# Hybrid layer on one core: the lower part of one weight piece per gate/up chunk by ScalarE and an adding DMA, other steps moved

## The chip, the core and the metric

The kernel runs on one core of a Trainium2 chip. TensorE (PE) multiplies 128x128 blocks, VectorE (DVE) and ScalarE (ACT) work on 128 partitions, GpSimd (POOL) and SyncE (SP) issue DMAs here. The metric is the device time of one execution in microseconds (us); lower is better. Times are compared as medians of several runs.

## The reference

One layer on 256 tokens of width 2048, all in float32: a feed-forward block, a mixer (retention heads and sparse attention beside each other), a second feed-forward block, each added to x, and a last norm. The part that fills most of the time is the feed-forward block, run twice with 5632 hidden columns:

```
def rmsnorm(x, g):
    y = xf * lax.rsqrt(jnp.mean(xf * xf, axis=-1, keepdims=True) + NORM_EPS)
    return (y * g.astype(jnp.float32)).astype(x.dtype)

def swiglu(h, w_gate, w_up, w_down):
    return (jax.nn.silu(h @ w_gate) * (h @ w_up)) @ w_down

x = x + 0.5 * swiglu(rmsnorm(x, ffn1_norm), ffn1_w_gate, ffn1_w_up, ffn1_w_down)
... mixer: rope on queries and keys, retention, top-64 attention, x + concat @ w_out
x = x + 0.5 * swiglu(rmsnorm(x, ffn2_norm), ...)
return rmsnorm(x, final_norm)
```

## The kernel before, in words

**Two parts of every number.** TensorE multiplies in a rounded form of float32. To keep the precision, every operand is held as an upper part `hi` (the rounded number, written by an ACT copy, L287) and a lower part `lo` (the number less `hi`, a DVE subtraction, L293). A product takes three matmuls: hi with hi, hi with lo, lo with hi.

**Pieces.** All weights stream from HBM in loads of 1 MB into three buffers `raw` (`load`, L259). A load is cut into pieces of at most 1024 columns; `split` (L268) makes `hi` and `lo` of one piece, and the matmuls of a piece follow. A feed-forward block is cut into chunks of 512 hidden columns; `wide` (L179) lists the pieces of one chunk, which hold gate and up side by side. A pair is 256 rows of the weights, one load. A plain pair (C) has two pieces and 24 matmuls. A pair of kind S replaces the 2x2 block product by seven products of sums: DVE first subtracts quarters of the raw weights in place (`less`, L278), and there are four pieces and 21 matmuls. A chunk is eight pairs. All chunks but the first of each block follow `UP` in the order `ORDER`, that is S C S C S C C C, with 22 pieces; there are 20 of them, five in each of the two parts of the two blocks. A down pass (`DOWN`) follows each part, in two halves.

**Order of the work.** The program fixes the order on every engine. The main loop (L1072 to L1085) goes over the pieces: at step i it runs the small tasks booked for that step (`after`, `run_step`; a task that yields n goes on n steps later), then splits piece i + 4, then issues the matmuls of piece i. `hi` and `lo` have five buffers each, so the split of a piece waits until the piece five before it has been multiplied. A load is issued when the buffer of the load three before it is free, which is when DVE has made the last `lo` of it.

**What is booked in a chunk.** Once the last S pair is multiplied, `sums_of` (L479) puts the seven products together: ACT copies bank M1, DVE adds M6 to it (L477); one step later the transposes of the chunk before go into M1 and M6 (`turn`, L563, with L567) and are split again; one step later DVE adds M5 and M7. Half a chunk's end later `ups` and `hidden` (L542, L550) add the plain products, apply silu on ACT and multiply.

**Other places that the change touches.** `tables` (L650) makes the sine and cosine tables on DVE and ACT during the first down pass and sends them through DRAM. `turn_early` (L592) transposes x at the end of the first block. `rstd` and `row_of` (L457, L439) turn the norm's factor into a row by a matmul with `diag`; `scaled_tables` (L710) multiplies the tables by it; `rope` (L731) uses them. `rg_done` (L813) makes the gates of the retention heads and `ret_mix` (L993) combines them with the heads' output for `w_out`. `FIRST` (L32) is the order of the pairs in the very first chunk, in which x is also scaled, transposed and split (`first_x`, and for S pairs `s_of_x`, L362).

Of the kernel before, what the change touches and what calls it, by code (L numbers as in the profile page):

```python
# [19 lines left out]
P = 128  # L20
# [8 lines left out]
UP = "CSCSCSCC"  # L29
ORDER = (1, 0, 3, 2, 5, 4, 6, 7)  # L30
PLAIN = "CCCCCCCC"
FIRST = (0, 2, 4, 6, 7, 1, 3, 5)  # L32
DOWN = ("SCSCSCSCCCCC", "SCSCSCSCCC")
NH = 8
NI = 16
# [16 lines left out]
def layer(ctx: ExitStack, tc: tile.TileContext, a: dict, out: bass.AP):  # L52
# [18 lines left out]
    def half_k(tag, bufs=2):  # L71
        return new(tmp, [P, 2, T], F32, tag, bufs)
# [35 lines left out]
    def after(step, fn):  # L108
        ends.setdefault(step, []).append(fn)
# [68 lines left out]

    def wide(src, plan, left, x0=False, tail=False, order=None, sums=SUM):  # L179

        start = len(pieces)
        seen, last = {}, {}
        ending = [[], []]
        s_end = None

        def mm(i, off, a, m, at=None, p=None):

            for n, (u, v) in enumerate(((0, 0), (0, 1), (1, 0))):
                st = m not in seen
                seen[m] = 1  # L190
                e = [i, off, (pieces[i]["pair"], a), m, u, v, st, False]
                last[m] = e
                pieces[i if at is None else at]["mms"].append(e)

        for at, p in enumerate(order or range(len(plan))):
            kind = plan[p]
            loads.append([(0, block(src, 2 * at, 2 * at + 2, 1024))])
            if x0:
                loads[-1] = [lambda p=p: load_xT(p)] + [(o, loads[-1][0][1][:, o:o + n]) for o, n in
                                                        ([(0, 512), (512, 512), (1024, 1024)] if at == 0 else [(0, 2048)])]  # L200
            i = len(pieces)
            if kind == "C":
                tiles = [(0, 1024), (1024, 1024)]
                if x0 and at == 0:
                    tiles = [(0, 512), (512, 512), (1024, 1024)]
            else:
                tiles = [(512, 1024), (1024, 1024), (0, 1024), (1536, 512)]
            for k, (off, n) in enumerate(tiles):
                pieces.append(dict(load=len(loads) - 1, off=off, n=n, mms=[], left=left, pair=p,
                                   sums=k if kind == "S" else None, x=[p] if x0 and k == 0 else []))  # L210
            if kind == "C":
                for c in (1, 0):
                    for k in range(2):
                        off = 1024 * (1 - c) + 512 * k
                        j = max(j for j, (o, n) in enumerate(tiles) if o <= off)
                        for t in range(2):
                            if tail and p >= len(plan) - 2:
                                ending[t].append((i + j, off - tiles[j][0], p, (t, k), sums[f"{t + 1}{c + 1}"]))
                                continue
                            mm(i + j, off - tiles[j][0], (t, k), sums[f"{t + 1}{c + 1}"])  # L220
            else:
                for k, off, a, m in S_BLOCKS:
                    mm(i + k, off, a, m)
                s_end = len(pieces)

        ending[1].sort(key=lambda e: e[4], reverse=True)
        for t in range(2):
            for i, off, p, a, m in ending[t]:
                mm(i, off, a, m, i if t == 0 else len(pieces) - 1)
        for e in last.values():  # L230
            e[7] = True
        return start, s_end, len(pieces) - 1, len(pieces)
# [22 lines left out]
        return len(pieces)  # L255

    n_loaded = [0]

    def load(i):  # L259
        raws[i] = new(wts, [P, 2048], F32, "raw", 3)  # L260
# [7 lines left out]
    def split(i):  # L268
        p = pieces[i]
        while n_loaded[0] < min(len(loads), p["load"] + 3):  # L270
            load(n_loaded[0])
            n_loaded[0] += 1
        for c in p.get("x", []):
            first_x(c, xT.pop(c))
        r = raws[p["load"]]
        raw = r[:, p["off"]:p["off"] + p["n"]]

        def less(a, b, o):  # L278
            V.tensor_tensor(r[:, o:o + 512], r[:, a:a + 512], r[:, b:b + 512], op=OP.subtract)  # L279


        k = p.get("sums")
        if k == 1:
            less(0, 1024, 1024)
        hi = new(wts, [P, 1024], F32R, "hi", BUFS)
        lo = new(wts, [P, 1024], F32R, "lo", BUFS)
        S.activation(hi[:, :p["n"]], raw, AF.Copy)  # L287
        if k == 1:
            less(0, 512, 0)
            less(512, 1024, 512)  # L290
        elif k == 2:
            less(1536, 512, 1536)
        V.tensor_tensor(lo[:, :p["n"]], raw, hi[:, :p["n"]].bitcast(F32), op=OP.subtract)  # L293
        split_of[i] = (hi, lo)


    def gain(norm, c, j):
# [141 lines left out]
    def row_of(tok):  # L439

        diag = new(tmp, [P, 2, P], F32, "diag", 1)
        for t in range(2):
            V.tensor_scalar(diag[:, t], ident, tok[:, t:t + 1], None, op0=OP.mult)
        ps = small()
        yield 2
        for t in range(2):
            TE.matmul(ps[:, t * P:(t + 1) * P], lhsT=ones, rhs=diag[:, t], start=True, stop=True)
        return ps[:, :T]
# [77 lines left out]
    def ffn(which, norm, next_norm, last):  # L526
        wgu, wd = a[f"wgu{which}"], [a[f"wd{which}{j}"] for j in range(2)]
        c = 0
        for part, n in enumerate(PARTS):
            hs = {}  # L530
            marks[which, part] = len(pieces)
            for cc in range(n):
                plain = c == 0
                start, s_end, half, end = wide(wgu[c], PLAIN if plain else UP, left_of(xg if plain else xs),
                                               plain and which == 1,
                                               order=ORDER if not plain else FIRST if which == 1 else None)
                u = {}

                if not plain:
# [51 lines left out]

    def turn_early(s_end, norm):  # L592

        for i, m in enumerate(("M1", "M5", "M6", "M7")):
            after(s_end + 2 + i, lambda i=i, m=m: turn_x(i, norm, m))

    def turn_late(end, norm, banks, later=0):
# [49 lines left out]

    rot_dram = new(dram, [P, 4, T], F32, "rot_dram")

    def tables():  # L650
        for k in range(2):
            ang, n = half_k("b"), half_k("sq")
            pi, pf = n[:, 0].bitcast(I32), n[:, 1]
            G.dma_start(pi, bass.AP(tensor=a["pos"].tensor, offset=a["pos"].offset, ap=[[0, P], [1, T]]))
            yield 4
            V.tensor_copy(pf, pi)
            for j in range(2):
                V.tensor_scalar(ang[:, j], pf, inv[:, k:k + 1], None, op0=OP.mult)
            yield 2
            V.tensor_scalar(n, ang, 1.0 / C_TWO_PI, None, op0=OP.mult)  # L660
            V.tensor_scalar(n[:, 0], n[:, 0], 0.25, None, op0=OP.add)
            yield 2
            V.tensor_scalar(n, n, MAGIC, None, op0=OP.add)
            V.tensor_scalar(n, n, MAGIC, None, op0=OP.subtract)
            for c in (C1, C2, C3):
                yield 2
                V.scalar_tensor_tensor(ang, n, -c, ang, op0=OP.mult, op1=OP.add)
            yield 1
            V.tensor_scalar(ang[:, 0], ang[:, 0], math.pi / 2, None, op0=OP.add)
            yield 1  # L670

            V.tensor_scalar(n, ang, 1.0 / C_TWO_PI, MAGIC, op0=OP.mult, op1=OP.add)
            V.tensor_scalar(n, n, MAGIC, None, op0=OP.subtract)
            for c in (C1, C2, C3):
                yield 2
                V.scalar_tensor_tensor(ang, n, -c, ang, op0=OP.mult, op1=OP.add)
            yield 2
            V.tensor_scalar(ang, ang, PI_DOWN, -PI_DOWN, op0=OP.min, op1=OP.max)
            yield 2
            S.activation(ang, ang, AF.Sin)  # L680
            yield 2
            V.tensor_scalar(ang[:, 1], ang[:, 1], sgn[:, k:k + 1], None, op0=OP.mult)
            G.dma_start(rot_dram[:, 2 * k:2 * k + 2], ang)
        yield 1
        act_table(AF.Silu)

    def load_tables():
        mix_ext()
# [12 lines left out]

    after(FIRST_SQ, first_squares)
    end = ffn(1, 0, 1, False)
    after(marks[1, 0, "down"] + 1, tables)
    after(marks[1, 1, "down"] + 4, load_tables)


# [6 lines left out]
        yield 2  # L714
        V.tensor_tensor(rot[:, :2], rot[:, :2], two(r_of[1]), op=OP.mult)

    after(m0 + 3, scaled_tables)

    heads = {}
    done_at = {}  # L720
# [26 lines left out]
    def cols(name, src, nchunks, idx=False, first=False):  # L747
# [7 lines left out]
        for c in range(nchunks):  # L755
            chunk = chunks[c]
            end = ends_[c] if c in ends_ else stream(src[c], kts, 256, 8, 4, rhs_x, chunk, mm_cols, 2)

            def done(chunk=chunk, c=c):
                if c % 2 == 0:  # L760
                    heads[name].append(big(shape=(P, 4, T)))
                return rope(chunk, 2, heads[name][c // 2][:, 2 * (c % 2):2 * (c % 2) + 2], idx,
                            3 if len(heads) == 1 and c == 0 else 1)

            after(end, done)
        done_at[name] = len(pieces)
# [42 lines left out]
    for c in range(4):  # L809
# [3 lines left out]
        def rg_done(chunk=chunk, c=c):  # L813
# [3 lines left out]
            s = half_k("s")  # L817
            S.activation(s, g, AF.Silu)
            gate[c] = s

        after(end, rg_done)
        rg_end.append(end)
# [213 lines left out]
    after(s + 6, ret_norm)  # L1036
    for n in range(2):
        after(s + 7 + n, lambda n=n: ret_scale(n))
    for c in range(4):
        after(max(rg_end[c] + 2, s + 10 + 2 * c), lambda c=c: ret_mix(c))  # L1040

    class MixIn:
# [129 lines left out]
```

## Time and profile before

| | |
|---|---|
| median of 3 runs | 1867.61 us (1867.21 to 1868.33) |
| the profiled execution | 1868.15 us, of it the span from first to last instruction 1866.3 us |
| PE busy | 98% of the span, 8643 matmuls |
| DVE busy | 88%, ACT 57%, POOL 0.4% |
| DMA | 360.51 MB, mean 193 GB/s |
| mean granted clock of PE | 0.997 |

An engine's idle time is shown before the instruction that it waited with, and the releaser is the instruction whose end let it go on. Busy times of PE are modelled: a matmul of 512 columns is drawn with 0.39 us, but such matmuls start 0.23 us apart.

### The profile page before, as it was taken

What the parts mean: (1) busy time and instruction counts of PE and PEld (TensorE: products, weight loads), DVE (VectorE), ACT (ScalarE), POOL (GpSimd) and SP (SyncE); (2) the same over time, 40 slices, a digit from 0 to 9 for tenths busy, and PEclk for the clock granted to TensorE, in tenths of its full rate; (3) what the DMA queues carried; (4) which work ended last, traced back from release to release, by engine and by line L of the source; (5) the groups of instructions that cost most, each with busy time, mean ns of one, the idle gap of its engine ahead of it and who ended that gap; (6) DMA issues with size and microseconds to landing.
All of it is one profiled execution on the core that took longest, in us unless ns stands there. A gap on an engine that the chain in (4) does not pass through costs nothing.

```text
span 1866.3 us, 22800 instructions
## 1 busy us (share of the span) xinstructions
PE 1836.9 (98%) x8643; PEld 1523.8 (82%) x8643; DVE 1646.2 (88%) x2122; ACT 1072.9 (57%) x1353; POOL 6.9 (0%) x17
## 2 busy tenths in 40 slices
PE   9999999999999999999999999999999999999997
PEld 7788787888888887988888888888888888888886
DVE  6999999999999997689865886799999889999997
ACT  7655655545565555656554566556555455555564
POOL 0000000000000000000000000000000000000000
PEclk9999999999999999999999999999999999999999
DMA  8545555565554544545434464555555555555454
GB/s 316 203 181 183 203 203 191 180 229 198 205 206 183 212 181 173 184 159 210 179 137 172 145 225 150 207 185 191 210 207 183 202 203 198 186 188 212 186 190 170
DMA packets 52237, 360.51 MB, mean 193 GB/s; under 512 B 5984, under 2 KB 5984, under 8 KB 9632
## 3 DMA queue, kind: packets, MB, share of 16 engines
q1 hardware_dynamic: 50976, 355.62, 51.6%
q0 software_dynamic: 576, 1.84, 0.3%
q10 hardware_dynamic: 576, 1.60, 0.3%
q8 instruction: 67, 1.10, 0.2%
q14 instruction: 42, 0.34, 0.1%
HBM read 356.42 MB, written 2.62 MB: 192 GB/s over the span
## 4 chain that ended last, share of the span: by engine, by line
PE 80%; DVE 12%; ACT 4%; issue 2%; DMA 2%; SPq 0%; ACTq 0%; DVEq 0%
PE M L236 63%; PE M L150 8%; DVE lo L293 7%; PE M L152 4%; DVE raw L279 2%; ACT hi L287 2%; PE M L168 1%; PE M L169 1%; PE M L167 1%; PE M L567 1%; DMA raw<-in_wgu 1%; DMA e<-in_xT 1%; DVE x L474 1%; ACT sq L416 0%; DVE e L477 0%
## 5 line engine op out<-in xcount | busy, mean ns | idle before, releaser
L287 ACT ACTIVATE hi<-raw 128x1024 fp32r<-128x1024 f32 (+2 forms) x859 | 844.6, 1006 | 561.5 <-DVE raw L279 359.5
L293 DVE TENSOR_TENSOR lo<-raw,hi 128x1024 fp32r<-128x1024 f32 (+2 forms) x859 | 976.4, 1159 | 122.1 <-ACT hi L287 108.7
L236 PE MATMUL M<-hi,xg 128*128 128x512 f32 x2240 | 725.5, 390 | 1.7 <-ACT e L546 1.5
L236 PE MATMUL M<-hi,mid 128*128 128x512 f32 x1690 | 527.4, 391 | 1.9 <-DVE e L1001 1.6
L236 PEld LDWEIGHTS M<-hi,xg 128*128 128x128 f32 x2240 | 420.5, 188 | 89.2 <-ACT e L546 1.9
L236 PE MATMUL M<-lo,xg 128*128 128x512 f32 x1120 | 437.9, 391 | 5.7 <-DVE lo L293 5.6
L236 PEld LDWEIGHTS M<-hi,mid 128*128 128x128 f32 x1690 | 317.2, 188 | 70.2 <-DVE e L1001 2.0
L236 PE MATMUL M<-lo,mid 128*128 128x512 f32 x845 | 329.8, 390 | 1.0 <-DVE lo L293 0.8
L279 DVE TENSOR_TENSOR raw<-raw 128x512 f32<-128x512 f32 x380 | 262.9, 692 | 12.7
L236 PEld LDWEIGHTS M<-lo,xg 128*128 128x128 f32 x1120 | 210.3, 188 | 55.5 <-DVE lo L293 12.7
L150 PE MATMUL M<-xg,hi 128*128 128x512 f32 x688 | 245.6, 401 | 0.4 <-DVE xg L307 0.3
L236 PEld LDWEIGHTS M<-lo,mid 128*128 128x128 f32 x845 | 158.6, 188 | 36.5 <-DVE lo L293 4.3
L152 PE MATMUL M<-xg,lo 128*128 128x256 f32 x645 | 180.9, 280 | 0.0
L150 PEld LDWEIGHTS M<-xg,hi 128*128 128x128 f32 x688 | 128.7, 189 | 30.3 <-issue 1.3
L236 PE MATMUL M<-hi,ext 128*128 128x512 f32 x360 | 141.2, 392 | 1.5 <-ACT s L557 1.4
L152 PEld LDWEIGHTS M<-xg,lo 128*128 128x128 f32 x645 | 122.3, 190 | 0.8
L236 PEld LDWEIGHTS M<-hi,ext 128*128 128x128 f32 x360 | 67.5, 188 | 18.9 <-DVE s L477 3.6
L236 PE MATMUL M<-lo,ext 128*128 128x512 f32 x180 | 70.1, 389 | 0.0
L477 DVE TENSOR_TENSOR s<-s,M 128x512 f32<-128x512 f32 x98 | 65.6, 683 | 1.9 <-PE M L236 0.9
L557 ACT ACTIVATE s<-s,r_tok 128x512 f32<-128x512 f32 x40 | 27.0, 718 | 53.5 <-DVE s L477 53.5
L477 DVE TENSOR_TENSOR e<-s,M 128x512 f32<-128x512 f32 x58 | 39.7, 684 | 1.0
L742 ACT ACTIVATE b<-e 64x512 f32<-64x512 f32 (+2 forms) x46 | 28.1, 612 | 19.8 <-DVE e L728 19.3
(176 smaller groups left out, 933.2 us busy)
## 6 DMA issues: line engine op xcount, KB each, us to landing
raw<-in_wgu SPq DMA_DIRECT2D x175, 1024.0 KB, 4.8
raw<-in_wd SPq DMA_DIRECT2D x88, 1024.0 KB, 4.8
raw<-in_w_out SPq DMA_DIRECT2D x16, 1024.0 KB, 4.9
raw<-in_w_iq SPq DMA_DIRECT2D x8, 1024.0 KB, 4.8
raw<-in_w_aq SPq DMA_DIRECT2D x8, 1024.0 KB, 4.7
raw<-in_w_rk SPq DMA_DIRECT2D x8, 1024.0 KB, 4.8
raw<-in_w_rq SPq DMA_DIRECT2D x8, 1024.0 KB, 4.7
raw<-in_w_rv SPq DMA_DIRECT2D x8, 1024.0 KB, 4.9
```

Source lines behind the costliest of these rows:

```text
L150: TE.matmul(acc, lhsT=hi[:, c:c + P], rhs=r, start=st, stop=sp)
L152: TE.matmul(acc[:, T:], lhsT=lo[:, c:c + P], rhs=r[:, :T], start=False, stop=False)
L167: TE.matmul(o, lhsT=h, rhs=hi[:, i * n:(i + 1) * n], start=st, stop=False)
L168: TE.matmul(o, lhsT=h, rhs=lo[:, i * n:(i + 1) * n], start=False, stop=False)
L169: TE.matmul(o, lhsT=l, rhs=hi[:, i * n:(i + 1) * n], start=False, stop=sp)
L236: TE.matmul(bank[m], lhsT=p["left"](pair, a)[u], rhs=split_of[i][v][:, off:off + 512], start=st, stop=sp)
L279: V.tensor_tensor(r[:, o:o + 512], r[:, a:a + 512], r[:, b:b + 512], op=OP.subtract)
L287: S.activation(hi[:, :p["n"]], raw, AF.Copy)
L293: V.tensor_tensor(lo[:, :p["n"]], raw, hi[:, :p["n"]].bitcast(F32), op=OP.subtract)
L477: V.tensor_tensor(o, a, b, op=OP.add)
L557: S.activation(u[b], bank[SUM[b]] if plain else u[b], AF.Silu, scale=r_tok[norm][:, t:t + 1])
L742: S.activation(b[p0:p0 + w], q[p1:p1 + w], AF.Copy)
```

## The change

In each S chunk of gate/up the last piece (21) gets its lower part in another way: while piece 18 is split, ACT writes the negative of the rounded piece into a tile `lower` and a POOL DMA adds the raw piece to it. DVE's subtraction of that piece is left out. Besides, the order `FIRST` is another; the early transposes of x take the banks in the order M1, M6, M7, M5; `row_of` waits three steps and the scaled tables begin a step later, and the first two `rope` chains with them; the tables are made in two tasks begun 24 and 53 steps into the down pass, with their DVE steps closer together and a switch back to silu's function table after each; `ret_mix(3)` is run by the task that makes its gate; and the DMA scratch is set to 4096.

```diff
-FIRST = (0, 2, 4, 6, 7, 1, 3, 5)
+FIRST = (0, 2, 1, 4, 3, 6, 5, 7)
...
+        if added:
+            pieces[-4]["lower"] = len(pieces) - 1
+            pieces[-1]["adds"] = True
...
-        lo = new(wts, [P, 1024], F32R, "lo", BUFS)
+        lo = lowers.pop(i) if p.get("adds") else new(wts, [P, 1024], F32R, "lo", BUFS)
...
-        V.tensor_tensor(lo[:, :p["n"]], raw, hi[:, :p["n"]].bitcast(F32), op=OP.subtract)
+        if not p.get("adds"):
+            V.tensor_tensor(lo[:, :p["n"]], raw, hi[:, :p["n"]].bitcast(F32), op=OP.subtract)
         split_of[i] = (hi, lo)
+        if p.get("lower"):
+            q = pieces[p["lower"]]
+            src = raws[q["load"]][:, q["off"]:q["off"] + q["n"]]
+            lowers[p["lower"]] = t = new(wts, [P, 1024], F32R, "lower", 1)
+            S.activation(t, src, AF.Copy, scale=-1.0)
+            G.dma_start(t, src, accum_op=OP.add)
...
@@ row_of
-        yield 2
+        yield 3
...
@@ ffn
+                                               added=not plain)
...
@@ turn_early
-        for i, m in enumerate(("M1", "M5", "M6", "M7")):
+        for i, m in enumerate(("M1", "M6", "M7", "M5")):
...
@@ tables: one task for each k; the waits between its steps
-    def tables():
-        for k in range(2):
+    def tables(k):
...
-            yield 2
-            S.activation(ang, ang, AF.Sin)
-            yield 2
+        yield 2
+        S.activation(ang, ang, AF.Sin)
         yield 1
         act_table(AF.Silu)
+        yield 1
+        V.tensor_scalar(ang[:, 1], ang[:, 1], sgn[:, k:k + 1], None, op0=OP.mult)
+        G.dma_start(rot_dram[:, 2 * k:2 * k + 2], ang)
...
-    after(marks[1, 0, "down"] + 1, tables)
+    for k in range(2):
+        after(marks[1, 0, "down"] + (24, 53)[k], lambda k=k: tables(k))
...
-    after(m0 + 3, scaled_tables)
+    after(m0 + 4, scaled_tables)
...
-                            3 if len(heads) == 1 and c == 0 else 1)
+                            (5, 4)[c] if len(heads) == 1 and c < 2 else 1)
...
@@ rg_done
             gate[c] = s
+            if c == 3:
+                ret_mix(c)
...
-    for c in range(4):
+    assert rg_end[3] + 1 >= s + 16
+    for c in range(3):
         after(max(rg_end[c] + 2, s + 10 + 2 * c), lambda c=c: ret_mix(c))
...
-    nc = bacc.Bacc("TRN2", target_bir_lowering=False, num_devices=1)
+    nc = bacc.Bacc("TRN2", target_bir_lowering=False, num_devices=1, dynamic_dma_scratch_size=4096)
```

## Rows read from the trace of the kernel before

**Rows 1.** The page's first part: an engine's busy time, share, instructions.
```profile
PE 1836.9 (98%) x8643; PEld 1523.8 (82%) x8643; DVE 1646.2 (88%) x2122; ACT 1072.9 (57%) x1353; POOL 6.9 (0%) x17
```

**Rows 2.** Waits of PE, whole span: who, for whom, us in total, times, longest.
```profile
PE M L236 <- DVE lo L293: 6.4, 19, 0.7
PE M L447 <- DVE diag L443: 2.4, 1, 2.4
PE M L567 <- DVE s L477: 2.0, 1, 2.0
PE M L236 <- DVE e L1001: 1.6, 1, 1.6
PE M L236 <- ACT e L546: 1.5, 1, 1.5
PE M L405 <- DVE e L477: 1.4, 1, 1.4
PE M L236 <- ACT s L557: 1.4, 1, 1.4
```

**Rows 3.** Timeline of PE: start, us; chunk starts (hi,ext), eight transposes.
```profile
98.05 0.39 PE L236 MATMUL M<-hi,ext 128*128 128x512 f32 x1
...
141.12 0.39 PE L236 MATMUL M<-hi,ext 128*128 128x512 f32 x1
...
441.84 0.39 PE L236 MATMUL M<-hi,ext 128*128 128x512 f32 x1
...
469.72 1.03 PE L567 MATMUL M<-ident,e 128*128 128x128 f32 x8
...
484.22 0.39 PE L236 MATMUL M<-hi,ext 128*128 128x512 f32 x1
```

**Rows 4.** Timeline of DVE in the chunk from 98.05, and at 311.
```profile
125.65 0.68 DVE L477 TENSOR_TENSOR s<-s,M 128x512 f32<-128x512 f32 x1
126.88 1.22 DVE L293 TENSOR_TENSOR lo<-raw,hi 128x1024 fp32r<-128x1024 f32 x1 [0.55 <-ACT hi L287]
...
309.63 0.69 DVE L676 SCALAR_TENSOR_TENSOR b<-sq,b 128x512 f32<-128x512 f32 x1
...
311.36 0.68 DVE L477 TENSOR_TENSOR s<-s,M 128x512 f32<-128x512 f32 x1
```

**Rows 5.** Timeline of ACT, the end of the first chunk and the same chunk.
```profile
55.51 1.28 ACT L557 ACT_TABLE_LOAD   x1
...
122.10 1.07 ACT L287 ACTIVATE hi<-raw 128x1024 fp32r<-128x1024 f32 x1 [0.29 <-PE M L236]
...
125.78 1.06 ACT L287 ACTIVATE hi<-raw 128x1024 fp32r<-128x1024 f32 x1 [0.82 <-DVE lo L293]
...
144.42 2.94 ACT L287 ACTIVATE hi<-raw 128x1024 fp32r<-128x1024 f32 x3
```

**Rows 6.** SP's issues of the eighth pair's load in two chunks, and the first's landing.
```profile
120.86 0.33 SPq L266 DMA_DIRECT2D raw<-in_wgu  x1
...
DMA to landing us min/median/max: 4.8/4.8/4.8
...
463.13 0.33 SPq L266 DMA_DIRECT2D raw<-in_wgu  x1
```

**Rows 7.** The chain of work over 95 to 150: start, us, what.
```profile
102.29 1.24 DVE lo L293
...
145.50 1.24 DVE lo L293
...
146.78 3.24 PE M L236 x13
```

**Rows 8.** The DMA issues: queue, count, KB each, median us to landing.
```profile
mid<-in_decay POOLq DMA_DIRECT2D x1, 512.0 KB, 6.1
```

**Rows 9.** Windows: us, then PE, PEld, DVE, ACT, POOL busy, PEclk, DMA share, GB/s.
```profile
742.00:746.00 4.00, 3.84 (x15) 3.42 (x16) 4.00 (x6) 2.15 (x3) 0.00 (x0) 0.57 0.35 121
...
310.00:312.10 2.10, 0.12 (x3) 0.00 (x1) 2.04 (x3) 0.61 (x1) 0.00 (x0) 1.00 0.97 375
```

More of the change, by code (lines that the diff above doesn't have):

```diff
@@ L177, in layer, with wide @@
         (3, 0, "A22", "M4"))
-    def wide(src, plan, left, x0=False, tail=False, order=None, sums=SUM):
+    def wide(src, plan, left, x0=False, tail=False, order=None, sums=SUM, added=False):
         start = len(pieces)
@@ L208, in wide @@
             for k, (off, n) in enumerate(tiles):
-                pieces.append(dict(load=len(loads) - 1, off=off, n=n, mms=[], left=left, pair=p,
+                pieces.append(dict(load=len(loads) - 1, off=off, n=n, mms=[], left=left, pair=p, lower=None, adds=False,
                                    sums=k if kind == "S" else None, x=[p] if x0 and k == 0 else []))
@@ L257, in layer @@
     n_loaded = [0]
+    lowers = {}
     def load(i):
@@ L535, in ffn @@
                                                plain and which == 1,
-                                               order=ORDER if not plain else FIRST if which == 1 else None)
+                                               order=ORDER if not plain else FIRST if which == 1 else None,
+                                               added=not plain)
                 u = {}
@@ L648, in layer @@
     rot_dram = new(dram, [P, 4, T], F32, "rot_dram")
-    def tables():
-        for k in range(2):
[L652 to L658, printed above, removed]
-            yield 2
-            V.tensor_scalar(n, ang, 1.0 / C_TWO_PI, None, op0=OP.mult)
-            V.tensor_scalar(n[:, 0], n[:, 0], 0.25, None, op0=OP.add)
-            yield 2
[L663 to L679, printed above, removed]
-            S.activation(ang, ang, AF.Sin)
-            yield 2
-            V.tensor_scalar(ang[:, 1], ang[:, 1], sgn[:, k:k + 1], None, op0=OP.mult)
-            G.dma_start(rot_dram[:, 2 * k:2 * k + 2], ang)
@@ new lines, in tables, with less_turns @@
+    def tables(k):
+        ang, n = half_k("b"), half_k("sq")
+        pi, pf = n[:, 0].bitcast(I32), n[:, 1]
+        G.dma_start(pi, bass.AP(tensor=a["pos"].tensor, offset=a["pos"].offset, ap=[[0, P], [1, T]]))
+        yield 2
+        def less_turns(c):
+            V.scalar_tensor_tensor(ang, n, -c, ang, op0=OP.mult, op1=OP.add)
+        V.tensor_copy(pf, pi)
+        for j in range(2):
+            V.tensor_scalar(ang[:, j], pf, inv[:, k:k + 1], None, op0=OP.mult)
+        yield 1
+        V.tensor_scalar(n, ang, 1.0 / C_TWO_PI, None, op0=OP.mult)
+        V.tensor_scalar(n[:, 0], n[:, 0], 0.25, None, op0=OP.add)
+        yield 1
+        V.tensor_scalar(n, n, MAGIC, None, op0=OP.add)
+        V.tensor_scalar(n, n, MAGIC, None, op0=OP.subtract)
+        yield 1
+        less_turns(C1)
+        less_turns(C2)
+        yield 1
+        less_turns(C3)
+        V.tensor_scalar(ang[:, 0], ang[:, 0], math.pi / 2, None, op0=OP.add)
+        yield 1
+        V.tensor_scalar(n, ang, 1.0 / C_TWO_PI, MAGIC, op0=OP.mult, op1=OP.add)
+        V.tensor_scalar(n, n, MAGIC, None, op0=OP.subtract)
+        yield 1
+        less_turns(C1)
+        less_turns(C2)
+        yield 1
+        less_turns(C3)
+        V.tensor_scalar(ang, ang, PI_DOWN, -PI_DOWN, op0=OP.min, op1=OP.max)
+        yield 2
+        S.activation(ang, ang, AF.Sin)
@@ L684, in tables @@
         yield 1
         act_table(AF.Silu)
+        yield 1
+        V.tensor_scalar(ang[:, 1], ang[:, 1], sgn[:, k:k + 1], None, op0=OP.mult)
+        G.dma_start(rot_dram[:, 2 * k:2 * k + 2], ang)
     def load_tables():
```

## The prediction, made before the changed kernel ran

> **What bounds the kernel now.** I read the page first, then TensorE's waits, then the timelines of one gate/up chunk engine by engine, and the chain of waits through it. TensorE is busy for 1836.9 us of the span [rows 1], so at most some 29 us can be won, and the waits name what of that has a cause [rows 2]: 16 of the 19 waits on `lo` L293 (0.34 us each, four in each run of five chunks) and six single waits of 1.4 to 2.4 us.
>
> A listed wait counts from a modelled end, so I price it from starts. A chunk with a wait takes 141.12 - 98.05 = 43.07 us, one without 484.22 - 441.84 = 42.38 us [rows 3]. One of the 16 costs 0.7 us, all of them 11 us.
>
> Where the wait comes from. I number the 22 pieces of a chunk 0 to 21 and count time from its first matmul (S0). DVE in the chunk from 98.05 ends the `lo` of piece 19 and issues the sum `s` L477 at 125.65, then stands idle 0.55 us until 126.88 [rows 4]. The cause stands in ACT's row: `hi` of piece 20 begins at 125.78 [rows 5], and piece 20 is the first of the eighth pair, whose load SP issued at 120.86 and which takes 4.8 us to land, at about 125.7 [rows 6]. So the eighth pair's load, issued when the `lo` of piece 15 has freed its buffer, lands just as it is needed. From there DVE works almost without a break to the `lo` at 145.50, of piece 4 of the next chunk, and with this one the chain crosses over to TensorE [rows 7].
>
> **The change, the wide chunks.** It takes one `lo` of 1.2 us per gate/up chunk from DVE (1.22 at 126.88 [rows 4], less an overlap), 20 times. It adds, behind `hi` of piece 18, an activation of 128x1024 on ACT (1.06 us, like `hi` [rows 5]) and a POOL DMA of 512 KB. That activation reads the eighth pair. ACT runs in order: `hi` of piece 18 begins at 122.10 and ends at 123.2 [rows 5], the load lands at 125.7, so ACT stands 2.5 us. Behind it queue `hi` of piece 19, the copy of M1 (L482) and `hi` of piece 20; on DVE behind `hi` 19 its `lo`, then the sum `s` L477 that reads bank M6; on TensorE the transposes L567 into M6, which must wait for that sum.
>
> From the landing L: 0.10 until ACT starts (125.68 to 125.78), the new activation 1.06, `hi` 19 1.06, its `lo` 1.22, the sum 0.68: 4.1, less about 0.1 of overlap between neighbours (three `hi` take 2.94 us, not 3.18 [rows 5]). The sum ends at L + 4.0. TensorE reaches the second four transposes 0.4 us after the first four (eight take 0.8), at 469.72 + 0.4 - 441.84 = S0 + 28.3 [rows 3]. L is S0 + 26.1 where DVE starts a chunk without arrears: 463.13 - 441.84 = 21.3 for the issue, 4.8 for the landing [rows 3, 6]. So TensorE waits 30.1 - 28.3 = 1.8 us in such a chunk.
>
> In the chunks that follow, DVE carries arrears. Its `lo` of piece 20 follows the sum and ends at L + 5.1. From there to the end of the `lo` of the next piece 4 took 146.7 - 128.1 = 18.6 us [rows 4, 7], now 1.2 less: L + 22.5. The next chunk starts (S0') at L + 4.0 + 14.1 (470.12 to 484.22 [rows 3]), so that `lo` ends at S0' + 4.4; TensorE wants it after the 22 matmuls of 0.23 us ahead of it, at S0' + 5.0, and the old wait is gone. From it to the end of `lo` 15, which SP's issue follows, DVE needs 120.86 - 103.53 = 17.3 us of back-to-back work [rows 6, 7]: issue at S0' + 21.7, landing at S0' + 26.4, and TensorE waits 30.4 - 28.3 = 2.1 us. Were the arrears to stay as they are now, the landing would be at 125.7 - 98.05 - 0.7 = S0 + 26.9 and the wait 2.6 us; both ends, 1.8 and 2.6, stay for the range.
>
> Transposes fall on the sum in 18 of the 20 chunks (the first chunk of each second part has none). Four first ones at 1.8, fourteen at 2.1, and 0.1 for the restart each: 38 us. Against it stand the 11 us of the old waits. Net +27 us.
>
> The adding DMA itself I cost at nothing. What hides it is the 14.4 us from the end of the new activation (L + 1.2) to TensorE's first use of piece 21's lower part (L + 4.0 + 0.4 + four pieces of 2.74 = L + 15.4, plus one matmul, 0.23). The trace shows no adding DMA. The nearest row is POOL's 512 KB from HBM, 6.1 us [rows 8]; reading the target too might double it, 12.2, still hidden. From below it can't gain. The bytes pass beside loads that are wanted 10 us later. Two queues meet it: POOL's own, where only the tables' four transfers stand, and SP's, where the load into the eighth pair's buffer now waits for this DMA and `hi` 21 instead of the `lo` of piece 21; it is wanted for piece 6 of the next chunk, after L + 20. The smaller scratch for POOL's descriptors changes no instruction; I cost it at nothing. By the Trainium skill (DMA: Bandwidth & Descriptors, section Anatomy of one DMA) a DMA of this queue takes 2.0 us plus its bytes at 436 GB/s, by estimate 3.2 us here; the sum would be the same, and [rows 8] show nearly twice that for this size.
>
> **The change, the single places.** Each is priced with what can be late next.
> - Tables: 312.1, TensorE waits 2.0 us for the sum L477 at 311.36, which stands on DVE behind table steps [rows 2, 4]. They move to the plain pairs of the down pass. Gain 2.2 with the restart. One more pair of function-table loads (1.28 us each [rows 5]) falls on ACT there, hidden by the four pieces that are split ahead; uncovered it is 2.6 us.
> - `row_of` one step later and begun one step later: the wait of 2.4 us for `diag` [rows 2] lets the clock down: 0.57 granted over 742 to 746, that is 0.43 x 4 = 1.7 us lost [rows 9]. Together 4.2; I take 3.8, since the next `lo` may be 0.4 late. The first two `rope` chains start later with it, after their banks have been copied out, so that no matmul waits for them.
> - x transposed by way of M6, M7, M5: the wait of 1.4 us at L405 is for the last sum on M5, now used last: 1.5.
> - `ret_mix(3)` one step earlier: its L1001 holds TensorE 1.6 us [rows 2]; it now stands a piece earlier in DVE's queue, ahead of one `lo` of 1.2 us, and its four transposes a piece earlier on TensorE: 1.7 with the restart.
> - FIRST: the pairs that need sums of x are prepared among the others, not last. The waits of 1.5 and 1.4 us (L546, L557 [rows 2]) come from ACT's backlog at the first chunk's end. Between 0 and 3.4 with restarts; the same work can now hold up pairs 2 and 4, so I take 2.0.
>
> Together -11.2 (from -6 to -13.4).
>
> **Sum** against the profiled execution (span 1866.3, time 1868.15): 1868.15 + 38 - 11 - 11.2 = 1884. That execution lies 0.5 us above the median of 1867.61; I forecast 1883. Bounds: 18 x 1.9 (restart in) = 34 less 13 (should 20 old waits end) less 13.4 gives +8, 1875; 18 x 2.7 = 49 less 8 (should a few of the old stay) less 6 gives +35, 1902.
>
> **Rivals.**
> - The lower part isn't in the way. Then DVE's 1.2 us come through: -11 - 11.2, 1845. It decides at a landing 2.1 us earlier in the chunk, or if the sum L477 stood ahead of `lo` 19. For it: ACT idles elsewhere in the chunk, and DVE's time is what the 16 waits lack. Against: `hi` 20 starts 0.1 us after the landing already, and the new activation reads the same load two pieces earlier. Chance 0.11.
> - The clock falls in each chunk. After the 2.4 us wait the clock fell; the 2.0 us wait at 310 to 312 left it at 1.00, its upper level of 2.4 GHz [rows 2, 9]. The new wait is split by four transposes, 1.2 and 0.9 us by the steps above. If it fell each time, 18 x 1.7 = 31 more, 1914. The Trainium skill (TensorE: Matmul & The Clock Gate, section HAM oscillation) has a kernel that waits once per tile and pays for the clock at each; by that rule it is this rival, and the row at 310 to 312 speaks against it so far. With it goes an adding DMA that takes over 14.4 us, 20 us for each us beyond. Chance of both 0.11.
> - The waits shrink to about 1.1 us (arrears taken up, transposes later) and the single places pay in full: no change, 1867. Against: every term of L + 4.0 is a row. Chance 0.04.
>
> **How the numbers follow.** The forecast holds 0.74, at 1875 to 1902. A difference under 0.2% (3.7 us) can't be told from none. Faster 0.11 (first rival), same 0.04 (third), slower 0.85 (forecast and second). The range 1866 to 1902 takes in the third and leaves out the first and most of the second, about 0.2.
>
> **What would show it.** Right: a new activation 20 times, each after some 2 us of idle ACT ended by a load; transposes L567 waiting for the sum L477 18 times, 1 to 2 us each; chunk starts 44.5 us apart instead of 43.1; waits on `lo` down from 19 to about 3; the clock at 1.00 throughout the chunks; the waits on `diag` and L1001 gone. Wrong: chunk starts 42.4 us apart, or TensorE waiting on POOL's DMA at piece 21.

## The result and the profile after

The changed kernel takes 1888.97 us (median, 1888.34 to 1890.69), beside 1867.58 us of the kernel before: ratio 1.0113, 95% interval 1.0101 to 1.0126, 21.4 us slower. The forecast was 1883. The profiled execution has a span of 1887.4 us, 21.1 more than before. Lines have moved: matmuls of the weights L236 are now L239, `hi` L287 is L291, `lo` L293 is L298, the sums L477 are L488, their copy on ACT is L493, the transposes L567 are L579; the new activation is L304, the adding DMA L305.

The page's first part, against [rows 1]: PE has the same work, DVE 20 operations and 24.2 us less, ACT 21 operations and 21.2 us more.

```profile
PE 1837.5 (97%) x8643; PEld 1524.6 (81%) x8643; DVE 1622.0 (86%) x2102; ACT 1094.1 (58%) x1374; POOL 24.5 (1%) x37
```

Waits of PE, against [rows 2]. The waits on `lo` are down from 19 to 5; `diag`, L1001, the old waits at L567 and L405 are gone; two groups of 18 have come, the first and the second four transposes of a chunk, and a wait of 4.2 us that the prediction doesn't have.

```profile
PE M L579 <- ACT s L493: 16.9, 18, 1.4
PE M L579 <- DVE s L488: 12.9, 18, 0.7
PE M L150 <- DVE xg L318: 4.2, 1, 4.2
PE M L239 <- DVE lo L298: 2.3, 5, 0.8
```

Waits of ACT: the new activation waits for the load each of the 20 times, 39.0 us in all.

```profile
ACT lower L304 <- DMA raw<-in_wgu: 39.0, 20, 2.4
```

One chunk of the changed kernel, by PE's timeline (start, busy us; in brackets the idle time before and who ended it). The chunk takes 144.09 - 99.65 = 44.44 us, before 43.07 [rows 3].

```profile
99.65 0.39 PE L239 MATMUL M<-hi,ext 128*128 128x512 f32 x1
...
128.59 0.66 PE L579 MATMUL M<-ident,e 128*128 128x128 f32 x4 [0.90 <-ACT s L493]
129.97 0.66 PE L579 MATMUL M<-ident,e 128*128 128x128 f32 x4 [0.72 <-DVE s L488]
...
144.09 0.39 PE L239 MATMUL M<-hi,ext 128*128 128x512 f32 x1
```

ACT in that chunk, against [rows 5]: `hi` of piece 18 at 123.02, then 1.96 us idle, the new activation, `hi` of piece 19, the copy, `hi` of piece 20.

```profile
123.02 1.07 ACT L291 ACTIVATE hi<-raw 128x1024 fp32r<-128x1024 f32 x1 [0.29 <-PE M L239]
126.05 1.06 ACT L304 ACTIVATE lower<-raw 128x1024 fp32r<-128x1024 f32 x1 [1.96 <-DMA raw<-in_wgu]
127.02 1.04 ACT L291 ACTIVATE hi<-raw 128x1024 fp32r<-128x1024 f32 x1
127.96 0.58 ACT L493 ACTIVATE s<-M 128x512 f32<-128x512 f32 x1
```

DVE, against [rows 4]: relieved of 1.2 us per chunk, it now stands 2.75 us at one place, since `lo` of piece 19 waits for ACT.

```profile
128.09 1.23 DVE L298 TENSOR_TENSOR lo<-raw,hi 128x1024 fp32r<-128x1024 f32 x1 [2.75 <-ACT hi L291]
129.23 0.68 DVE L488 TENSOR_TENSOR s<-s,M 128x512 f32<-128x512 f32 x1
129.83 1.22 DVE L298 TENSOR_TENSOR lo<-raw,hi 128x1024 fp32r<-128x1024 f32 x1
```

The chain of waits over 120 to 150, against [rows 7]: what crossed to PE from a `lo` now starts at a load and crosses at the transposes.

```profile
121.23 4.74 DMA raw<-in_wgu
...
126.05 0.04 ACT lower L304
...
127.02 1.05 ACT hi L291
...
129.23 0.69 DVE s L488
129.92 0.04 issue
129.97 0.66 PE M L579 x4
130.62 16.36 PE M L239 x72
```

The clock (windows; PEclk is the third number from the right), against [rows 9]: 1.00 behind the waits of that chunk, and half behind the wait of 4.2 us, which stands at the first matmul of the mixer. Behind the waits of the other 17 chunks it is 1.00 too.

```profile
129.00:133.00 4.00, 3.28 (x19) 2.59 (x18) 3.87 (x9) 2.59 (x5) 0.00 (x0) 1.00 1.03 245
735.60:739.10 3.50, 3.24 (x10) 2.76 (x11) 3.04 (x5) 1.58 (x2) 0.00 (x0) 0.51 0.20 30
```

```profile
735.86 0.80 PE L150 MATMUL M<-xg,hi 128*128 128x512 f32 x1 [4.17 <-DVE xg L318]
```

### The profile page after: what moved, and what is told of

It is laid out like the page before. It is cut to its first block, busy times and chain, and to the rows that moved or that the text cites. A ratio compares the mean times of both kernels' runs of the same rounds, so it can differ in the third digit from the quotient of the medians.

```text
span 1887.4 us, 22919 instructions
## 1 busy us (share of the span) xinstructions
PE 1837.5 (97%) x8643; PEld 1524.6 (81%) x8643; DVE 1622.0 (86%) x2102; ACT 1094.1 (58%) x1374; POOL 24.5 (1%) x37
## 4 chain that ended last, share of the span: by engine, by line
PE 61%; DVE 25%; DMA 6%; issue 4%; ACT 3%; ACTq 0%; SPq 0%; DVEq 0%
PE M L239 42%; DVE lo L298 14%; PE M L150 9%; DVE raw L283 7%; DMA raw<-in_wgu 5%; PE M L152 4%; ACT hi L291 2%; PE M L168 1%; PE M L169 1%; PE M L167 1%; DVE s L488 1%; DVE x L485 1%; PE M L579 1%; ACT sq L427 0%; DVE e L488 0%
## 5 line engine op out<-in xcount | busy, mean ns | idle before, releaser
L291 ACT ACTIVATE hi<-raw 128x1024 fp32r<-128x1024 f32 (+2 forms) x859 | 849.9, 1008 | 519.1 <-DVE raw L283 327.1
L298 DVE TENSOR_TENSOR lo<-raw,hi 128x1024 fp32r<-128x1024 f32 (+1 forms) x839 | 953.2, 1157 | 168.4 <-ACT hi L291 155.4
L239 PE MATMUL M<-hi,xg 128*128 128x512 f32 x2240 | 726.0, 390 | 1.2 <-DVE x L485 0.8
L239 PE MATMUL M<-hi,mid 128*128 128x512 f32 x1690 | 527.3, 390 | 0.3
L239 PEld LDWEIGHTS M<-hi,xg 128*128 128x128 f32 x2240 | 420.5, 188 | 89.4 <-ACT hi L291 1.4
L239 PE MATMUL M<-lo,xg 128*128 128x512 f32 x1040 | 405.0, 389 | 1.8 <-DVE lo L298 1.8
L239 PEld LDWEIGHTS M<-hi,mid 128*128 128x128 f32 x1690 | 317.2, 188 | 68.0 <-DVE x L485 2.3
L239 PE MATMUL M<-lo,mid 128*128 128x512 f32 x845 | 329.6, 390 | 0.6 <-DVE lo L298 0.5
L239 PEld LDWEIGHTS M<-lo,xg 128*128 128x128 f32 x1040 | 195.3, 188 | 42.5 <-DVE lo L298 2.7
L239 PEld LDWEIGHTS M<-lo,mid 128*128 128x128 f32 x845 | 158.7, 188 | 35.3 <-DVE lo L298 3.0
L239 PE MATMUL M<-hi,ext 128*128 128x512 f32 x360 | 140.3, 390 | 0.8 <-ACT s L569 0.6
L239 PEld LDWEIGHTS M<-hi,ext 128*128 128x128 f32 x360 | 67.6, 188 | 15.6 <-ACT s L569 1.0
L239 PE MATMUL M<-lo,ext 128*128 128x512 f32 x180 | 70.0, 389 | 0.0
L488 DVE TENSOR_TENSOR s<-s,M 128x512 f32<-128x512 f32 x98 | 65.4, 683 | 2.2 <-PE M L239 1.2
L579 PE MATMUL M<-ident,e 128*128 128x128 f32 x176 | 27.7, 284 | 29.8 <-ACT s L493 16.9
L569 ACT ACTIVATE s<-s,r_tok 128x512 f32<-128x512 f32 x40 | 27.0, 719 | 49.5 <-DVE s L488 49.5
L579 PEld LDWEIGHTS M<-ident,e 128*128 128x128 f32 x176 | 18.8, 140 | 42.1 <-ACT s L493 22.6
```

The costliest lines, as they stand in the source:

```text
L239: TE.matmul(bank[m], lhsT=p["left"](pair, a)[u], rhs=split_of[i][v][:, off:off + 512], start=st, stop=sp)
L488: V.tensor_tensor(o, a, b, op=OP.add)
L569: S.activation(u[b], bank[SUM[b]] if plain else u[b], AF.Silu, scale=r_tok[norm][:, t:t + 1])
L579: TE.transpose(v[:, j, t * P:(t + 1) * P], ht[t][:, halves(2 * q + j, P)], ident)
```

## The experiments

Each was timed beside the kernel before on its chip; "us slower" or "faster" of two kernels is the difference of medians. The kernel before has medians from 1867.58 to 1868.52 us there.

**The lower part alone**: the kernel before with `wide`, `split`, `lowers` and the scratch size of the change, all else as before.

> The kernel before with the lower part by ACT and the adding DMA alone; FIRST, tables, bank order, row_of, ret_mix as before. Theory (ACT stands before the new activation until the eighth pair's load lands, and the sum L477 and the transposes stand behind it): 18 waits of 2.0 us less the 16 old ones of 0.7 us, +25 us, 1893 us, chunk starts 44.5 us apart. Rival (the moved single places made the changed kernel slower): 1868 or below, chunk starts 42.4 us apart.

Measured 1895.23 us, ratio 1.0142 (1.0127 to 1.0157), 26.7 us slower than before on its chip. 18 chunks with a wait on each half of the transposes; chunks 44.1 to 44.6 us apart.

**The single places alone**: the change without its lower part.

```diff
-                                               added=not plain)
+                                               added=False)
```

> The changed kernel with DVE's subtraction back in every piece, all single places as changed. Theory: 1889 less 25, 1864 us, chunk starts 43.1 us apart, old waits on lo back. The single places then bring 4 us in place of the 11 forecast, because the wait of 4.2 us at the mixer's first matmul stays. Rival (single places at fault): 1885 or more.

Measured 1863.74 us, ratio 0.9974 (0.9964 to 0.9984): 4.8 us faster than before. So the lower part costs 1888.97 - 1863.74 = 25.2 us beside the other edits, or 21.4 + 4.8 = 26.2 us with each kernel against the kernel before on its own chip (1867.58 and 1868.52), and 26.7 us without them (forecast 27). The single places give 4.8 where the forecast had 11.2.

**One piece ahead instead of three**: the new activation stands behind `hi` of piece 20, the first of the same load.

```diff
-            pieces[-4]["lower"] = len(pieces) - 1
+            pieces[-2]["lower"] = len(pieces) - 1
```

> The changed kernel with the activation and the adding DMA behind the upper part of piece 20 (one piece ahead) in place of piece 18. Piece 20 waits for the same load anyway, so by the theory nothing new waits: 18 x 2.0 less, 1852 us, chunk starts 42.4 us apart, if the DMA (4.7 us) lands in the 9 us that are left. Rival (the adding DMA itself costs, by its bytes beside the loads or by landing late): 1885 or more, with waits at piece 21.

Measured 1851.40 us, ratio 0.9907 (0.9892 to 0.9922): 37.6 us faster than the change, by one index. No transpose waits, and chunks take 139.42 - 97.03 = 42.39 us, PE's own time. The adding DMA lands later than in the change, and neither PE nor ACT nor DVE waits for it. SP does, with the load that takes the eighth pair's buffer next, and in the chunks no engine waits for that load in turn (DMA issues, last number median us to landing, and waits of SP; the change first, then this kernel):

```profile
lower<-raw POOLq DMA_DIRECT2D x20, 512.0 KB, 4.7
SPq L270 <- DMA lower<-raw: 52.1, 20, 3.1
```

```profile
lower<-raw POOLq DMA_DIRECT2D x20, 512.0 KB, 6.5
SPq L270 <- DMA lower<-raw: 157.6, 20, 9.1
```

**Another piece, of a load long landed**: piece 19 gets the lower part, behind `hi` of piece 18.

```diff
-            pieces[-4]["lower"] = len(pieces) - 1
-            pieces[-1]["adds"] = True
+            pieces[-4]["lower"] = len(pieces) - 3
+            pieces[-3]["adds"] = True
```

> The changed kernel with piece 19 in place of piece 21 given to ACT and the adding DMA, still begun behind the upper part of piece 18. As many activations and DMAs of the same size at the same place, but they read the seventh pair's load, which has landed by then. Theory (the wait for the load is the whole cause): 1852 us, chunk starts 42.4 us apart, no idle ACT before the activation. Rival (the added activation, or the DMA, at that place is what delays the sum): between 1870 and 1889.

A miss: 1862.78 us, ratio 0.9971 (0.9961 to 0.9982). The block is gone, but so is the relief: 21 waits on `lo`, 7.5 us, and chunks 43.1 us apart, as without any lower part. DVE's time isn't worth the same at every place of a chunk. Relieved of `lo` of piece 19, DVE waits for the copy of M1 and then for `hi` of piece 20, and starts on the transposes' result (L333) at 126.72, 29.94 us behind the chunk's start at 96.78, as before the change (128.02 - 98.05 = 29.97):

```profile
124.29 0.69 DVE L488 TENSOR_TENSOR s<-s,M 128x512 f32<-128x512 f32 x1 [1.15 <-ACT s L493]
125.57 1.23 DVE L298 TENSOR_TENSOR lo<-raw,hi 128x1024 fp32r<-128x1024 f32 x1 [0.60 <-ACT hi L291]
126.72 0.28 DVE L333 TENSOR_TENSOR sq<-b 128x128 f32<-128x128 f32 x1
```

**The block without the relief**: the change, but nothing reads what the new activation writes, and DVE makes the lower part of piece 21.

```diff
-            G.dma_start(t, src, accum_op=OP.add)
```

> The changed kernel with the new activation at its place behind hi of piece 18, but without the adding DMA: nothing reads what the activation writes, and the lower part of piece 21 is written by VectorE again as in the kernel before. It has the block and not the relief. Theory (the loop through the landing of the eighth pair: landing, lo of piece 20, lo of the next piece 4, lo of its piece 15, the next landing): lo of piece 20 ends at L + 5.1 as in the changed kernel, lo of the next piece 4 at L + 23.7, of its piece 15 at L + 41.0, the next landing at L + 45.8; so chunks start 45.7 to 45.8 us apart instead of 44.45, the waits on lo are back, and with 1863.7 us for the change without its lower part the time is 1863.7 + 18 x 2.6 = 1910 us. Rival (the block costs TensorE its 2.1 us and the relief gives its 0.7 us, each by itself): 1889 + 16 x 0.7 = 1900 us, chunks 45.1 us apart.

Measured 1911.39 us, ratio 1.0234 (1.0219 to 1.0250); 13 chunk distances (without the very first and the two whose chunk has no transposes) average 45.66 us. The loop holds, the plain addition (1900) doesn't. One thing was not expected: in 6 of the 18 chunks PE's clock fell behind the transposes. PE's timeline and windows, a chunk without the fall and the next one, with it:

```profile
174.64 0.66 PE L578 MATMUL M<-ident,e 128*128 128x128 f32 x4 [1.33 <-ACT s L492]
176.01 0.66 PE L578 MATMUL M<-ident,e 128*128 128x128 f32 x4 [0.72 <-DVE s L487]
...
220.29 0.66 PE L578 MATMUL M<-ident,e 128*128 128x128 f32 x4 [1.31 <-ACT s L492]
221.67 0.86 PE L578 MATMUL M<-ident,e 128*128 128x128 f32 x4 [0.72 <-DVE s L487]
```

```profile
174.60:179.00 4.40, 3.64 (x19) 2.97 (x20) 4.27 (x9) 3.00 (x5) 0.00 (x0) 1.00 0.58 194
222.00:225.00 3.00, 3.00 (x10) 2.41 (x9) 2.87 (x8) 1.61 (x4) 0.00 (x0) 0.50 0.85 322
```

Such a chunk takes 47.3 to 47.5 us and the next, where the trace gives its length, 44.0 to 44.3. Without a fall in the chunk or in the one before it, a chunk takes 45.69 to 45.76 us (three of them; 45.26 and 45.28 where the one before has no transposes, 44.01 at the second block's start). So most of what the clock costs is taken from the next chunk's waits, which fits a pace set by DVE's loop and not by PE.

**Four buffers for the loads**, all instructions in place, with the lower part and without it.

```diff
-        raws[i] = new(wts, [P, 2048], F32, "raw", 3)
+        raws[i] = new(wts, [P, 2048], F32, "raw", 4)
```

> The changed kernel with four buffers for the loaded weights instead of three; every instruction stays in its place. The eighth pair's load then takes the buffer that lo of piece 11 frees, not that of piece 15, so it can be issued some 5 us earlier in the chunk. Theory: the landing ends both waits; with it more than 2.1 us earlier ScalarE isn't held behind hi of piece 18, the sum on bank M6 is early enough, and the chunks start 42.4 us apart: 1851 us, from 1850 to 1854. Rival: the new activation itself (1.06 us ahead of hi of piece 19, whenever its data come) makes the sum late: chunks of 43 us or more, 1862 to 1875.

Measured 1850.01 us, ratio 0.9906 (0.9891 to 0.9921). With the data there, the activation stands at the same place in ACT's queue and starts without a wait, and all eight transposes follow each other (ACT's timeline, then PE's):

```profile
120.70 1.04 ACT L304 ACTIVATE lower<-raw 128x1024 fp32r<-128x1024 f32 x1
121.65 1.04 ACT L291 ACTIVATE hi<-raw 128x1024 fp32r<-128x1024 f32 x1
```

```profile
124.25 1.03 PE L579 MATMUL M<-ident,e 128*128 128x128 f32 x8
```

> The changed kernel without its lower part (1863.7 us with three buffers), with four buffers for the loaded weights. Theory: what the old waits on lo lacked was not VectorE's time as such (busy 41.4 of 43.1 us in a chunk) but the landing of the eighth pair, which holds VectorE up in the middle of its backlog; with the landing earlier VectorE runs through and the chunks start 42.4 to 42.6 us apart: 1852 to 1855 us. Rival: VectorE lacks the time itself; the waits on lo stay and the chunks take 43.1 us: 1862 to 1865 us.

The theory missed, the rival held: 1860.75 us, ratio 0.9962 (0.9949 to 0.9975), 20 waits on `lo`, chunks 43.1 us apart with the landing out of the way. (The 3.0 us gained over three buffers lie elsewhere, among other places at the start of chunk 6, where PE no longer waits for x.) In this kernel DVE waits 0.42 us at 169.42 for the copy of the transposes' result. From there it works with no break over 0.15 us to the sums at 183.87. ACT's L569 waits for these, `hi` of piece 4 starts as L569 ends, `lo` of piece 4 follows that `hi` and ends 18.7 us after 169.42, and PE waits for this `lo`. DVE idles 0.20 us for L569 and 0.15 us for `hi`; so even without these two the `lo` would come only 0.3 us sooner, and PE's own pace (42.39 us a chunk) would have it 0.7 us sooner. DVE's timeline, then ACT's and PE's:

```profile
169.42 0.29 DVE L333 TENSOR_TENSOR sq<-b 128x128 f32<-128x128 f32 x1 [0.42 <-ACT b L348]
...
183.87 1.28 DVE L488 TENSOR_TENSOR s<-s,M 128x512 f32<-128x512 f32 x2
185.34 1.42 DVE L572 SCALAR_TENSOR_TENSOR e<-e,r_tok,s 128x512 f32<-128x512 f32 x2 [0.20 <-ACT s L569]
186.90 2.36 DVE L298 TENSOR_TENSOR lo<-raw,hi 128x1024 fp32r<-128x1024 f32 x2
```

```profile
184.58 1.34 ACT L569 ACTIVATE s<-s,r_tok 128x512 f32<-128x512 f32 x2 [2.84 <-DVE s L488]
185.83 2.94 ACT L291 ACTIVATE hi<-raw 128x1024 fp32r<-128x1024 f32 x3
```

```profile
188.18 0.50 PE L239 MATMUL M<-lo,xg 128*128 128x512 f32 x1 [0.30 <-DVE lo L298]
```

So the old wait is a loop from the transposes through DVE's work behind them, with a short way through ACT at its end, to that `lo`. What is taken from DVE ahead of the transposes' result (piece 19) only lengthens its waits there; what is taken behind it (piece 21) shortens the loop.

**The single places**, on the kernel with the activation one piece ahead (1851.40 us). First the order of the early transposes, M5 ahead of M7:

```diff
-        for i, m in enumerate(("M1", "M6", "M7", "M5")):
+        for i, m in enumerate(("M1", "M6", "M5", "M7")):
```

> The kernel with the new activation two pieces later (1851.4 us), with one edit: x is transposed early by way of M1, M6, M5, M7 instead of M1, M6, M7, M5. Theory: the 4.2 us wait at the mixer's first matmul is for bank M5, which the mixer's first pair of accumulators takes and which the early transposes now leave last; with M7 last, which only the second pair takes, that wait goes, and with it the drop of the clock behind it (1.7 us). Since TensorE then comes some 4 to 6 us earlier to the matmuls that read diag and to the last xg, 1 us may come back there: 1846.5, from 1845.5 to 1848. Rival: the wait is for what DVE has to do before the mixer in any order, so it moves to another place in the first 10 us of the mixer: 1850 to 1852.

Measured 1847.73 us, ratio 0.9889 (0.9873 to 0.9906), 3.7 us faster. The first matmul of the mixer no longer waits; 1.1 us come back 15 us later, at a part of x that is transposed late, and the clock stays at 1.00 (PE's timeline, windows):

```profile
712.33 0.50 PE L150 MATMUL M<-xg,hi 128*128 128x512 f32 x1
...
727.26 0.50 PE L150 MATMUL M<-xg,hi 128*128 128x512 f32 x1 [1.10 <-DVE xg L318]
```

```profile
727.00:731.00 4.00, 3.68 (x19) 2.99 (x20) 2.45 (x5) 3.17 (x5) 0.00 (x0) 1.00 0.55 229
```

Then, on this kernel, four edits undone or moved. `row_of`, the tables' scaling and the `rope` chains at their old places:

> As e5_bank_order, with row_of, the scaled tables and the first rope chains at their old places (yield 2, m0 + 3, waits 3 and 1). Theory: with TensorE no longer held up ahead of the mixer, the matmuls that read diag come before DVE has written it, as in the kernel before (a wait of 2.4 us and a drop of the clock, 1.7 us): 3 to 4 us slower than e5_bank_order. Rival: the later place of row_of is worth nothing, because DVE has the diag ready in either case: the same within 1 us.

Measured 1850.75 us (ratio 0.9907, 0.9892 to 0.9921), 3.0 us slower. The wait on `diag` is back, and behind it the lower clock; the stretch from the mixer's first such matmul to its last takes 338.56 us against 334.39, 4.2 more (waits of PE, windows):

```profile
PE M L458 <- DVE diag L454: 2.4, 1, 2.4
```

```profile
732.00:736.00 4.00, 3.61 (x16) 3.19 (x17) 3.95 (x6) 2.38 (x4) 0.00 (x0) 0.73 0.31 78
```

The old FIRST:

> As e5_bank_order, with the old order of the first chunk's pairs, FIRST = (0, 2, 4, 6, 7, 1, 3, 5). Theory: the first chunk took 45.8 us with the old order and 43.3 to 43.9 with the new one, against which the new order starts up to 0.9 us later: 1.6 to 2.5 us slower than e5_bank_order. Rival: what the old order loses in the chunk it saves ahead of it: the same within 0.7 us.

Measured 1849.89 us (0.9902, 0.9887 to 0.9916), 2.2 us slower, as the theory says; chunk 1, the first with S pairs, takes 45.68 us against 43.28.

The second set of table steps 11 pieces earlier:

> As e5_bank_order, with the second set of table steps begun 42 pieces into the down pass instead of 53. Theory: the steps that now stand on DVE among the last sums and additions to x before chunk 6 (its first part took 42.9 to 43.0 us against 41.5 in the kernel before) are over by then, and the wait for x at chunk 6's start goes: 1 to 1.5 us faster than e5_bank_order. Rival: the wait comes from the plain chunk's own pieces (the sums of x and the x additions stand there anyway), or the steps hold up an earlier piece instead: the same within 0.5 us.

A miss: 1850.50 us (0.9905, 0.9889 to 0.9919), 2.8 us slower. The wait for x at chunk 6 does go (that chunk takes 41.5 us again), but the steps now stand among the `lo` of S pairs, and three waits of PE on `lo` of 0.9 to 1.5 us come at 363 to 370. Waits of PE on `lo` in this kernel (2.0 us, 4 times, in the one it is compared with):

```profile
PE M L239 <- DVE lo L298: 5.6, 8, 1.5
```

`ret_mix(3)` at its old step:

> e5_bank_order (1847.7 us) with ret_mix(3) at its old step. Theory: TensorE waits 1.6 us again for its last operation on VectorE, which stands behind one more lo: 1.5 to 1.9 us slower. Rival: TensorE comes earlier or later here than in the kernel before, by what else was changed ahead of it, and the step is worth nothing: the same within 0.5 us.

A miss by its median: 1847.48 us (0.9892, 0.9876 to 0.9909), the same. The wait is back, 1.7 us, and two waits on `lo` just behind it (0.3 and 0.2 us) are gone:

```profile
PE M L239 <- DVE e L1019: 1.7, 1, 1.7
PE M L239 <- DVE lo L298: 0.7, 1, 0.7
```

The stretch from the mixer's last matmul to the second block's first chunk takes 135.35 us against 134.74, 0.6 us more. The median doesn't show it, because this kernel starts chunk 1, in the profiled execution, 1.3 us earlier (52.17 against 53.45), where nothing was edited. Differences of about a microsecond between two such kernels can come from there.

## Why the prediction was right, and where it wasn't

**The wide chunks held, term by term.** The landing is at 125.97, S0 + 26.3 (forecast S0 + 26.4); the sum ends at 129.23 + 0.68 = 129.91, L + 3.9 (forecast L + 4.0); the second four transposes start at S0 + 30.3 (30.4); chunks start 44.44 us apart (44.5); 18 chunks pay. Net +25.2 to +26.7 us against +27. That the load's landing behind a queue in order is what costs is shown from three sides: later in the queue (37.6 us faster than the change), earlier landing (39.0 us faster), block without relief (22.4 us slower). The adding DMA cost nothing, as costed, neither with 14.5 us to its first use here nor with some 11.5 us one piece ahead. Its landing, medians of 4.7 to 6.7 us over the kernels, lies inside the bounds. The estimate by the Trainium skill (DMA: Bandwidth & Descriptors, section Anatomy of one DMA), 3.2 us, was low; the measurement decides. No table load was added either: ACT has 11 in both kernels, and the pair that I priced as hidden does not exist.

**The mis-sized term is the single places**: -11.2 forecast, -4.8 measured, and this 6.4 us is more than the whole miss (21.4 measured, 16 forecast against the profiled execution). The step that failed most is "the wait of 1.4 us at L405 is for the last sum on M5, now used last: 1.5". I asked what the transposes wait for, not who takes the banks after them. The mixer's first matmuls accumulate in M5 and M6; with M5 transposed and emptied last they wait 4.2 us, and the clock falls behind that: +2.8 us in place of -1.5. PE's starts in the kernel before and in the change without the lower part put a number to each place (us):

| stretch | before | without lower part | difference | forecast |
|---|---|---|---|---|
| start to chunk 2 (FIRST) | 98.05 | 96.42 | -1.6 | -2.0 |
| chunk 5 to chunk 7 (tables) | 214.36 | 212.82 | -1.5 | -2.2 |
| chunk 10 to the mixer's first matmul (bank order) | 152.58 | 155.41 | +2.8 | -1.5 |
| to the mixer's last such matmul (`row_of`) | 337.02 | 334.16 | -2.9 | -3.8 |
| to the second block's first chunk (`ret_mix`) | 135.26 | 134.64 | -0.6 | -1.7 |

The rows add up to -3.8, much as the two spans differ (1866.3 and 1862.6). The first row carries a scatter at the start: four kernels with the same code up to there begin chunk 1 between 52.17 and 53.45. That chunk by itself takes 45.81 us before and 43.29 without the lower part, 2.5 less.

The tables win 3.0 at their old place and lose 1.5 at chunk 6, where the second set now ends. `row_of` wins only its wait: the clock that it was to save is 0.50 at 722.5 to 726 in the kernel without the lower part, behind the wait of the mixer's first matmul. With the bank order mended, `row_of` is worth 3.0 by the medians and 4.2 by its stretch, and FIRST 2.2 and 2.4, near their terms; `ret_mix` is worth 0.6 by its stretch, which the medians don't show.

**A reading that was right in its use and wrong in its reason.** I gave the eighth pair's landing as the cause of the old waits on `lo`. Four buffers take the landing away and the waits stay. DVE starts its work on the transposes' result at S0 + 29.97 in the chunk of [rows 4] (128.02) and at S0 + 29.86 with four buffers: the landing and the transposes' result come within 0.1 us of each other, and with the landing gone the transposes bind at almost the same time. The term (-11 us) came out because piece 21 lies behind both; that the reading named only one of two limits did no harm to the number, by luck.

**The rivals.** That the lower part isn't in the way is refuted as the change stands, and true with the activation two pieces later or the load earlier, which is the condition that it named. The falling clock did not come in the profiled execution. One of the four timed executions took 1890.69 us at a mean granted clock of 0.994, the other three 1888.34 to 1889.24 at 0.996 and 0.997; no trace shows whether the clock fell in some of its chunks. The kernel with the block alone shows how near it was: of its 12 chunks with a first wait of 1.3 to 1.6 us, each with a second wait of about 0.7, 6 were followed by the low clock and 6 were not; of the 6 chunks with a first wait of 0.5 to 0.7 us none was, nor any here, with 0.6 to 1.1 us (1.4 in the first). I read the rule of the Trainium skill (TensorE: Matmul & The Clock Gate, section HAM oscillation), a price at each tile that waits, as one for waits of any length; the kernel on that page waits some 3 to 5 us at each tile, longer than any wait of these chunks, so it decides nothing here. The row that I set against it, 310 to 312 [rows 9], covers the wait itself; behind it, over 312 to 316, the clock is 1.00 too. That the waits shrink to 1.1 us is refuted: 44.44 - 42.39 = 2.05 us per chunk.

**What stays open**: why the adding DMA lands in 4.7 us in one place and 6.5 in another; why the same waits cost the clock in one chunk and not in another; and why the stretch through the mixer's matmuls is no shorter (334.4 us against 333.6) once its clock stays up; none of these was tried. The fastest version is the one with the activation one piece ahead and M5 ahead of M7, 1847.73 us (1847.48 with `ret_mix(3)` at its old step, which is the same), 1.1% faster than before.

## What to carry to other kernels

Here an instruction moved early into ACT's queue started when its data were there, and everything behind it waited as long: compare the landing with the place in the queue before asking what the instruction costs. Relief of a busy engine counted here only behind the point from which its loop with the bound engine runs; find that point by the wait that ends last in one period. When the order of buffers is changed, follow each to its next user, not only to the wait that is removed.

## What the runs showed of the hardware

A POOL DMA that adds 512 KB from one SBUF tile into another landed in 4.7 to 6.7 us (medians of 20) beside the weight loads, which kept their 4.8 us median. Two waits of the same lengths on PE (1.3 and 0.7 us, four transposes between) were followed by the lower clock in one chunk and not in another (220.29 and 174.64 in the kernel with the block alone).
